# A Mamba-2 and stick-breaking encoder on one core: the SSD stage with GpSimd's tensor operations moved to VectorE, both PSUM halves added directly, and the RMS scale on ScalarE

## The chip, the cores and the metric

The kernel runs on one core of one Trainium2 chip. The metric is device time of one execution in microseconds (us), as the median of several executions. The engines have short names in the profile: PE is TensorE's matmuls, PEld its weight loads, DVE is VectorE, ACT is ScalarE, POOL is GpSimd, SP is SyncE, which issues most of the transfers. Each engine works through its own queue in order.

## The reference, cut to what matters

One sequence of 512 tokens, width 1024, two layers, all in float32. Layer 0 is a Mamba-2 mixer (the SSD stage) and a squared-ReLU MLP; layer 1 is stick-breaking attention and another MLP; each of the four sub-layers ends in a LayerNorm of `alpha * h + sublayer(h)`. The change touches only the mixer:

```python
y_diag = jnp.einsum("bcgls,bcgrls,bcsgrp->bclgrp", cb, decay_mat, xc)
...
y_off = jnp.einsum("bclgn,bcgrpn,bcgrl->bclgrp", cc, prev, jnp.exp(a_cs))
return (y_diag + y_off).reshape(b, l, h, p).astype(x.dtype)
...
y = (y + xh * d_skip[:, None]).reshape(b, l, D_INNER)
yg = (y * jax.nn.silu(z)).astype(jnp.float32).reshape(b, l, SSM_GROUPS, D_INNER // SSM_GROUPS)
yg = yg * lax.rsqrt(jnp.mean(jnp.square(yg), axis=-1, keepdims=True) + RMS_EPS)
y = (yg.reshape(b, l, D_INNER) * norm_w.astype(jnp.float32)).astype(u.dtype)
return y @ w_out
```

There are 8 groups of 4 heads with 64 channels each, so a group has 256 channels.

## The kernel before, in words

**Precision.** TensorE multiplies in a rounded float32 type. To keep float32 accuracy every operand is split into a high part (a cast) and a low part (the rest), and a product is three matmuls: high by high, low by high, high by low (`mm3`, L206 to L209). So every operand costs a cast, mostly on ScalarE, and a subtraction, mostly on VectorE. Weights arrive as tiles of 128x1024 through SP's queue; `emit_w` casts them on ScalarE (`wh`, L190) and subtracts (`wl`, L192). While `extra[3]` is set, every fourth weight's subtraction (`i % 4 == 1`) goes to GpSimd and the others to VectorE. `extra[3]` is set from the start of the program until attention begins.

**The SSD stage** (`ssm`) walks over the 8 groups. The projections of the next group (`in_bc`, `in_x`: tiles `pB`, `pC`, `px`) and of this group's gate (`in_z`: `pz`) are cut into small steps, which `fill.run` strews between the steps of this group's scan. The scan has four chunks of 128 tokens. For a chunk c:
- `decays`: GpSimd masks the log decays (`dm`, L771), TensorE sums them (`sg`), ScalarE exponentiates (`dec`, L777).
- `scores`: the C-by-B products `cb`, evicted by ScalarE (`cbm`, L787) and masked by GpSimd (L788).
- `front`: `dec` times `cbm` (L799), on VectorE for chunks 0 to 2 and on GpSimd for chunk 3; the split into `W` high and low (L801, L802); the chunk's state `st`; the running state `prev` times the block decay on GpSimd (L810), plus `st` on VectorE (L812); its split `pr` (L815, L816).
- `back`: the contribution of the state `po`, scaled by VectorE into `yg` (L831), plus the skip term `dx` on GpSimd (L832); the diagonal product `py`, in two halves of 256 columns side by side in one PSUM tile; ScalarE copies the second half to SBUF (`yl`, L840), GpSimd adds it to `yg` (L841), VectorE adds the first half from PSUM (L842).
- `gate` multiplies by silu(z) on VectorE (L847) and squares with a row sum on ScalarE (`ss`, L848). `finish` makes the reciprocal root on GpSimd (L856, L857), scales the four chunks of `yg` on VectorE (L859), transposes them on TensorE (`pyt`, L864) and splits the result into `yT` (L867, L868).

After groups 3 and 7 the output projection `so` runs in `tok_out` (L298 and L300 add it into the residual `v`). After the stage come MLP, attention and the second MLP.

**What sets the order.** The source order is only an input: the framework schedules every engine's queue by a timeline model of its own, over the whole program, and then puts in the semaphore waits. A change of a few instructions can therefore move others. PSUM has two sets of four buffers, `bg` for the scan's tiles and `mm` for projections.

Of the kernel before, what the change touches and what calls it, by code (L numbers as in the profile page):

```python
# [11 lines left out]
F32 = mybir.dt.float32  # L12
F32R = mybir.dt.float32r
AF = mybir.ActivationFunctionType
ALU = mybir.AluOpType
PSUM = bass.MemoryType.PSUM

P = 128
# [17 lines left out]
def trunk(ctx: ExitStack, tc: tile.TileContext, io):  # L36
    nc = tc.nc
# [7 lines left out]
    def psum(tag, shape, name):  # L45
        return ps.tile(shape, F32, tag=tag, name=name, bufs=4)
# [7 lines left out]
    def f(x):  # L54
        return x.bitcast(F32)
# [85 lines left out]
    marks.append(len(stream))  # L141
    ready = []
    taken = [0]
    extra = [None, 0, 0, True, 0]
    alt = {}
    sums = {}
    depth = [2]
# [58 lines left out]
    def mm3(out, a, b, start, stop, skip=False):  # L206
        nc.tensor.matmul(out, a[0], b[0], start=start, stop=False, skip_group_check=skip)  # L207
        nc.tensor.matmul(out, a[0], b[1], start=False, stop=False, skip_group_check=skip)  # L208
        return nc.tensor.matmul(out, a[1], b[0], start=False, stop=stop, skip_group_check=skip)  # L209
# [355 lines left out]
    def ssm(sp, nxt_ln):  # L565
# [33 lines left out]
        S4 = [P, 4, P]  # L599

        def pair(name, shape, tag, bufs):
            return tuple(sp.tile(shape, F32R, tag=tag + s, name=name + s, bufs=bufs) for s in "hl")
# [77 lines left out]
        def v3(t):  # L680
            return t.rearrange("p (h d) -> p h d", h=4)
# [111 lines left out]
        def front(q, c):  # L793
            g = q.g
            hs = slice(4 * g, 4 * g + 4)
            nm = f"{g}_{c}"
            dec = q.dec[c]
            eng = nc.gpsimd if c == 3 else nc.vector
            eng.tensor_tensor(dec, dec, q.cbm[:, c, :].unsqueeze(1).to_broadcast(S4), op=ALU.mult)  # L799
            W = q.W[c] = pair(f"W{nm}", S4, "W", 2)  # L800
            nc.scalar.copy(W[0], dec)  # L801
            nc.vector.tensor_sub(W[1], dec, f(W[0]))  # L802
            if c < NT - 1:
                pst = psum("bg", [P, 256], f"st{nm}")
                mm3(pst, (q.bt[0][:, c, :], q.bt[1][:, c, :]), (q.xe[0][:, c, :], q.xe[1][:, c, :]), True, True)
                if c == 0:
                    q.prev = sp.tile([P, 256], F32, tag="prev", name=f"pv{nm}", bufs=1)
                    nc.vector.tensor_copy(q.prev, pst)
                else:
                    nc.gpsimd.tensor_tensor(v3(q.prev), v3(q.prev),  # L810
                                            bdec[:, c, hs].unsqueeze(2).to_broadcast([P, 4, HP]), op=ALU.mult)
                    nc.vector.tensor_add(q.prev, pst, q.prev)  # L812
                nprev = q.prev
                pr = q.pr[c + 1] = pair(f"pr{nm}", [P, 256], "pr", 2)
                nc.scalar.copy(pr[0], nprev)  # L815
                nc.vector.tensor_sub(pr[1], nprev, f(pr[0]))  # L816

        def back(q, c):
            g = q.g
            hs = slice(4 * g, 4 * g + 4)  # L820
            cs = slice(c * P, (c + 1) * P)
            nm = f"{g}_{c}"
            if c == 0:
                q.yg = sp.tile([P, NT, 256], F32, tag="yg", name=f"yg{g}", bufs=1)
                q.ss = sp.tile([P, NT], F32, tag="ss", name=f"ss{g}", bufs=2)
            W, pr = q.W[c], q.pr[c]
            yc = q.yg[:, c, :]
            if c > 0:
                po = psum("bg", [P, 256], f"po{nm}")
                mm3(po, (q.C[0][:, cs], q.C[1][:, cs]), pr, True, True)  # L830
                nc.vector.tensor_tensor(v3(yc), v3(po), E[:, c, hs].unsqueeze(2).to_broadcast([P, 4, HP]), op=ALU.mult)  # L831
                nc.gpsimd.tensor_add(yc, yc, q.dx[:, c, :])  # L832
            py = psum("bg", [P, 4, 2, HP], f"py{nm}")
            for h in range(4):
                xh = q.xd[:, c, h, :, :].rearrange("p s d -> p (s d)")
                ph = py[:, h, :, :].rearrange("p s d -> p (s d)")
                nc.tensor.matmul(ph, W[0][:, h, :], xh, start=True, stop=False)
                nc.tensor.matmul(py[:, h, 0, :], W[1][:, h, :], q.xd[:, c, h, 0, :], start=False, stop=True)
            yl = sp.tile([P, 256], F32, tag="yl", name=f"yl{nm}", bufs=1)
            nc.scalar.copy(v3(yl), py[:, :, 1, :])  # L840
            nc.gpsimd.tensor_add(yc, yl, yc if c > 0 else q.dx[:, c, :])  # L841
            nc.vector.tensor_tensor(v3(yc), py[:, :, 0, :], v3(yc), op=ALU.add)  # L842

        def gate(q, c):
            nm = f"{q.g}_{c}"
# [4 lines left out]
        def finish(q, parts=1):  # L850
            g, yg = q.g, q.yg
            n = NT // parts
            for i in range(parts):
                cs = range(i * n, i * n + n)
                ss = q.ss[:, i * n:i * n + n]
                nc.gpsimd.tensor_scalar(ss, ss, 1.0 / 256.0, RMS_EPS, ALU.mult, ALU.add)  # L856
                nc.gpsimd.tensor_tensor(ss, ss, mhalf.to_broadcast([P, n]), op=ALU.pow)  # L857
                for c in cs:
                    nc.vector.tensor_scalar(yg[:, c, :], yg[:, c, :], q.ss[:, c:c + 1], None, ALU.mult)  # L859
                for j in range(2):  # L860
                    kt = 2 * g + j
                    pt = psum("bg", [P, n * P], f"pyt{g}{j}{i}")
                    for ci, c in enumerate(cs):
                        nc.tensor.transpose(pt[:, ci * P:(ci + 1) * P], yg[:, c, j * P:(j + 1) * P], ident)  # L864
                    ts_ = slice(i * n * P, (i + 1) * n * P)
                    oh, ol = yT[0][:, kt % 8, ts_], yT[1][:, kt % 8, ts_]
                    nc.scalar.activation(oh, pt, AF.Copy, scale=nw[:, kt:kt + 1])  # L867
                    nc.vector.scalar_tensor_tensor(ol, pt, nw[:, kt:kt + 1], f(oh), ALU.mult, ALU.subtract)  # L868
# [16 lines left out]
        for g in range(G):  # L885
# [3 lines left out]
            q = cur  # L889
# [7 lines left out]
            scores(q)  # L897
            fill.run(4)
            front(q, 0)
            fill.run(5)  # L900
            front(q, 1)
            fill.run(5)
            back(q, 0)
            fill.run(4)
            front(q, 2)
            fill.run(4)
            back(q, 1)
            fill.run(4)
            front(q, 3)
            fill.run(4)  # L910
            back(q, 2)
            fill.run(4)
            back(q, 3)
# [5 lines left out]
            if nxt:  # L919
                decays(nxt)  # L920
            finish(q, 1 if nxt else 2)
            if g == G - 1:
                def in_xd(i):
# [356 lines left out]
```

## Time and profile before

| what | value |
|---|---|
| three timed executions | 1426.99, 1427.30 (the median) and 1427.46 us |
| the profiled execution, and its span from first to last instruction | 1426.79 us, 1424.7 us |
| TensorE busy | 1394.1 us, 98% of the span |
| VectorE busy | 1078.2 us, 76% |
| ScalarE busy | 783.9 us, 55% |
| GpSimd busy | 221.4 us, 16% |
| mean granted TensorE clock | 0.994 of full speed |

The profile is one execution. A row of a group gives line, engine, operation, output and inputs, shape, count, then the engine's busy time, the mean time of one in ns, and the idle time of the engine before it with what ended it. A row of the timeline gives start and length. Matmuls are pipelined, so their lengths overlap, and the distance from one start to the next is what a matmul costs. GpSimd's work lies in the first 450 us, which are the SSD stage; after that it is nearly idle.

### The profile page before, as it was taken

The numbers are of one execution on the slowest core, as the hardware profiler recorded it, in microseconds if no ns is written. First come the engines' busy times: TensorE is split into PE (matmuls) and PEld (weight loads), VectorE is DVE, ScalarE is ACT, GpSimd is POOL, SyncE is SP. The second block draws the span as 40 slices with busy tenths as digits, with TensorE's granted clock in tenths as the row PEclk, the third lists the DMA queues.
The fourth block names the chain that finished last, engine by engine and source line by source line (L and its number), as shares of the span: only waits on it lengthen the run. The fifth ranks groups of instructions, "written<-read, shape, count | busy, mean of one in ns | idle before, by whom it ended". The sixth has DMA issues, their size and how long they took to land. (4 is left out here: it accounts for less than half of the span.)

```text
span 1424.7 us, 19323 instructions
## 1 busy us (share of the span) xinstructions
PE 1394.1 (98%) x7414; PEld 1199.9 (84%) x7414; DVE 1078.2 (76%) x1530; ACT 783.9 (55%) x1264; POOL 221.4 (16%) x249
## 2 busy tenths in 40 slices
PE   9999999999999999999999899999999999999996
PEld 6898897889997988888888789899878888888885
DVE  5798898368877695876849868787867876858587
ACT  5556574246653453626345468898842735454453
POOL 2344555135443100000000200000000000000001
PEclk9999999999999999999999999999999999999999
DMA  5223212221223356455443421121223455454533
GB/s 185 75 77 131 75 60 75 89 89 60 75 75 104 125 157 179 132 179 161 148 148 120 146 89 38 52 75 45 89 75 118 131 165 162 149 175 136 176 111 126
DMA packets 46699, 162.99 MB, mean 114 GB/s; under 512 B 5520, under 2 KB 5776, under 8 KB 46608
## 3 DMA queue, kind: packets, MB, share of 16 engines
q1 hardware_dynamic: 44016, 157.44, 35.4%
q10 hardware_dynamic: 2592, 4.33, 1.0%
q8 instruction: 58, 0.95, 0.3%
q14 instruction: 33, 0.27, 0.1%
HBM read 159.65 MB, written 2.10 MB: 114 GB/s over the span
## 5 line engine op out<-in xcount | busy, mean ns | idle before, releaser
L190 ACT CAST wh<-wr 128x1024 fp32r<-128x1024 f32 x235 | 246.7, 1050 | 328.5 <-DMA wr<-w 165.1
L192 DVE TENSOR_TENSOR wl<-wr,wh 128x1024 fp32r<-128x1024 f32 x218 | 268.4, 1232 | 184.3 <-ACT wh L190 182.9
L208 PE MATMUL f<-ln_hl,wh 128*128 128x512 f32 (+1 forms) x544 | 201.2, 371 | 0.0
L209 PE MATMUL f<-ln_hh,wl 128*128 128x512 f32 (+1 forms) x544 | 201.1, 370 | 0.0
L207 PE MATMUL f<-ln_hh,wh 128*128 128x512 f32 (+1 forms) x544 | 200.4, 371 | 0.0
L208 PEld LDWEIGHTS f<-ln_hl,wh 128*128 128x128 f32 x544 | 102.3, 188 | 17.6 <-DVE ln_hl L399 0.2
L209 PEld LDWEIGHTS f<-ln_hh,wl 128*128 128x128 f32 x544 | 102.3, 188 | 17.4
L207 PEld LDWEIGHTS f<-ln_hh,wh 128*128 128x128 f32 x544 | 101.9, 188 | 17.5
L347 POOL TENSOR_TENSOR ln_rs<-ln_sums 128x1 f32<-128x1 f32 (+1 forms) x6 | 3.1, 523 | 635.3 <-ACT lnr L345 635.3
L208 PE MATMUL X<-wl,hP 128*128 128x512 f32 x192 | 74.7, 389 | 0.0
L207 PE MATMUL X<-wh,hP 128*128 128x512 f32 x192 | 74.7, 389 | 0.0
L209 PE MATMUL X<-wh,l 128*128 128x512 f32 x192 | 74.2, 390 | 0.2 <-DVE l L460 0.2
L209 PE MATMUL pz<-wh,x_l 128*128 128x256 f32 x256 | 72.8, 284 | 0.0
L208 PE MATMUL pz<-wl,x_h 128*128 128x256 f32 x256 | 72.6, 284 | 0.0
L207 PE MATMUL pz<-wh,x_h 128*128 128x256 f32 x256 | 72.5, 283 | 0.0
L459 ACT CAST hP<-r 128x512 fp32r<-128x512 f32 x80 | 48.1, 620 | 32.4 <-DVE r L471 31.5
L192 POOL TENSOR_TENSOR wl<-wr,wh 128x1024 fp32r<-128x1024 f32 x17 | 42.5, 2503 | 93.3 <-ACT wh L190 92.9
L207 PE MATMUL px<-x_h,wh 128*128 128x512 f32 x128 | 50.8, 397 | 0.0
L208 PE MATMUL px<-x_l,wh 128*128 128x512 f32 x128 | 50.2, 393 | 0.0
L209 PE MATMUL px<-x_h,wl 128*128 128x512 f32 x128 | 50.2, 392 | 0.0
L208 PE MATMUL Y<-wl,hP 128*128 128x512 f32 x128 | 49.8, 389 | 0.0
L208 PEld LDWEIGHTS pz<-wl,x_h 128*128 128x128 f32 x256 | 48.7, 190 | 0.9
(1365 smaller groups left out, 3930.7 us busy)
## 6 DMA issues: line engine op xcount, KB each, us to landing
wr<-w SPq DMA_DIRECT2D x160, 512.0 KB, 3.6
wr<-w_bc SPq DMA_DIRECT2D x16, 512.0 KB, 3.6
wr<-w_x SPq DMA_DIRECT2D x16, 512.0 KB, 3.6
wr<-w_z SPq DMA_DIRECT2D x16, 512.0 KB, 3.5
wr<-w_so SPq DMA_DIRECT2D x16, 512.0 KB, 3.6
rawa<-w SPq DMA_DIRECT2D x16, 512.0 KB, 3.6
rawc<-w SPq DMA_DIRECT2D x16, 512.0 KB, 4.5
wr<-w_qk SPq DMA_DIRECT2D x16, 512.0 KB, 3.6
```

Source lines behind the costliest of these rows:

```text
L190: nc.scalar.copy(hi, raw)
L192: eng.tensor_sub(lo, raw, f(hi))
L207: nc.tensor.matmul(out, a[0], b[0], start=start, stop=False, skip_group_check=skip)
L208: nc.tensor.matmul(out, a[0], b[1], start=False, stop=False, skip_group_check=skip)
L209: return nc.tensor.matmul(out, a[1], b[0], start=False, stop=stop, skip_group_check=skip)
L347: nc.gpsimd.tensor_add(rs, self.sq[:, t0:t1, 0], self.sq[:, t0:t1, 1])
L459: nc.scalar.copy(h, src)
```

## The change

Six edits. GpSimd's share of the weight subtractions, the product for chunk 3, the decay of the running state and the addition of the skip term go to VectorE. The second half of `py` is no longer copied to SBUF and added by GpSimd: VectorE adds both halves from PSUM, the first one together with what stood in `yg` (or `dx` in chunk 0). The RMS scale of `yg` goes from VectorE to ScalarE. GpSimd keeps the masks (L771, L788) and the reciprocal root.

```diff
-    extra = [None, 0, 0, True, 0]
+    extra = [None, 0, 0, False, 0]
...
-            eng = nc.gpsimd if c == 3 else nc.vector
-            eng.tensor_tensor(dec, dec, q.cbm[:, c, :].unsqueeze(1).to_broadcast(S4), op=ALU.mult)
+            nc.vector.tensor_tensor(dec, dec, q.cbm[:, c, :].unsqueeze(1).to_broadcast(S4), op=ALU.mult)
...
-                    nc.gpsimd.tensor_tensor(v3(q.prev), v3(q.prev),
+                    nc.vector.tensor_tensor(v3(q.prev), v3(q.prev),
                                             bdec[:, c, hs].unsqueeze(2).to_broadcast([P, 4, HP]), op=ALU.mult)
...
-                nc.gpsimd.tensor_add(yc, yc, q.dx[:, c, :])
+                nc.vector.tensor_add(yc, yc, q.dx[:, c, :])
...
-            yl = sp.tile([P, 256], F32, tag="yl", name=f"yl{nm}", bufs=1)
-            nc.scalar.copy(v3(yl), py[:, :, 1, :])
-            nc.gpsimd.tensor_add(yc, yl, yc if c > 0 else q.dx[:, c, :])
-            nc.vector.tensor_tensor(v3(yc), py[:, :, 0, :], v3(yc), op=ALU.add)
+            nc.vector.tensor_tensor(v3(yc), py[:, :, 0, :], v3(yc if c > 0 else q.dx[:, c, :]), op=ALU.add)
+            nc.vector.tensor_tensor(v3(yc), py[:, :, 1, :], v3(yc), op=ALU.add)
...
-                    nc.vector.tensor_scalar(yg[:, c, :], yg[:, c, :], q.ss[:, c:c + 1], None, ALU.mult)
+                    nc.scalar.activation(yg[:, c, :], yg[:, c, :], AF.Copy, scale=q.ss[:, c:c + 1])
```

The number of matmuls stays at 7,414, but the scheduler orders most of the stage anew. Line numbers of the changed kernel are one lower than before from L799 to L838 and three lower from L847 on; its two additions of `py` are L838 and L839.

**VectorE at the start of the program.** `x_l` is the low part of the input x (eight tiles), `wl` that of a weight. Before:

```order
L577 TENSOR_TENSOR wdtlo<-wdt,wdthi 128x8x32
L590 TENSOR_TENSOR x_l<-xf,x_h 128x512
L192 TENSOR_TENSOR wl_130<-wr_127,wh_129 128x1024
L590 TENSOR_TENSOR x_l<-xf,x_h 128x512 x7
L192 TENSOR_TENSOR wl_238<-wr_235,wh_237 128x1024
```

With the change:

```order
L577 TENSOR_TENSOR wdtlo<-wdt,wdthi 128x8x32
L590 TENSOR_TENSOR x_l<-xf,x_h 128x512
L192 TENSOR_TENSOR wl_130<-wr_127,wh_129 128x1024
L590 TENSOR_TENSOR x_l<-xf,x_h 128x512 x3
L192 TENSOR_TENSOR wl_139<-wr_136,wh_138 128x1024
L590 TENSOR_TENSOR x_l<-xf,x_h 128x512 x4
L192 TENSOR_TENSOR wl_238<-wr_235,wh_237 128x1024
```

The weight `wl_139`, which GpSimd made before, now stands between the fourth and the fifth `x_l`.

**TensorE at the same place.** `pdt` and `pB` use x tile by tile, `pC` uses the weight 138/139. Before:

```order
L207 MATMUL pC_290<-x_h,wh_138 128x512
L208 MATMUL pC_290<-x_l,wh_138 128x512
L207 MATMUL pdt<-x_h,wdthi 128x512
L207 MATMUL pB_241<-x_h,wh_129 128x512
L208 MATMUL pdt<-x_l,wdthi 128x512
L209 MATMUL pdt<-x_h,wdtlo 128x512
```

With the change:

```order
L207 MATMUL pC_290<-x_h,wh_138 128x512
L208 MATMUL pC_290<-x_l,wh_138 128x512
L207 MATMUL pdt<-x_h,wdthi 128x512
L207 MATMUL pB_241<-x_h,wh_129 128x512
L209 MATMUL pC_290<-x_h,wl_139 128x512
L207 MATMUL pC_290<-x_h,wh_138 128x512
```

Where `pdt` asked for the fifth `x_l`, `pC` now goes on with the new weight: eleven matmuls of `pC` come before the next one that needs the fifth `x_l`.

**VectorE at the end of group 3,** just ahead of the output projection. `py_3` is the diagonal product of chunk 3, `pxt` the transposed x of group 4, `sz` the gate. Before:

```order
L842 TENSOR_TENSOR yg_2117<-py_3_2339,yg_2117 128x256
L847 TENSOR_TENSOR yg_2117<-yg_2117,sz_2318 128x256
L192 TENSOR_TENSOR wl_2546<-wr_2543,wh_2545 128x1024
L672 SCALAR_TENSOR_TENSOR ca_x_2407<-px_2382,cw,ca_x_2407 128x511
L859 TENSOR_SCALAR yg_2117<-yg_2117,ss_2118 128x256 x4
L672 SCALAR_TENSOR_TENSOR ca_x_2407<-px_2382,cw,ca_x_2407 128x510
L672 SCALAR_TENSOR_TENSOR ca_x_2407<-px_2382,cw,ca_x_2407 128x509
L729 TENSOR_TENSOR dx_2416<-pxt_2417,hv 128x512
L732 TENSOR_TENSOR xt_2423<-pxt_2417,dt 128x512
```

With the change:

```order
L838 TENSOR_TENSOR yg_2093<-py_3_2309,yg_2093 128x256
L192 TENSOR_TENSOR wl_2574<-wr_2571,wh_2573 128x1024
L729 TENSOR_TENSOR dx_2384<-pxt_2385,hv 128x512
L732 TENSOR_TENSOR xt_2391<-pxt_2385,dt 128x512
L839 TENSOR_TENSOR yg_2093<-py_3_2309,yg_2093 128x256
L729 TENSOR_TENSOR dx_2384<-pxt_2398,hv 128x512
L732 TENSOR_TENSOR xt_2404<-pxt_2398,dt 128x512
L844 TENSOR_TENSOR yg_2093<-yg_2093,sz_2288 128x256
```

The gate of the last chunk (L847 before, L844 now) stands behind the work on both `pxt` tiles; before it stood ahead of them, and so did the scale. On TensorE, the last `py_3` is followed before the change by 89 matmuls of 512 columns and the eight transposes of `pxt` until the first `pyt`, and with it by 26 and the same eight: first the four into the first `pxt` tile, then ten of the 26, then the four into the second, then the other 16.

## The prediction

> **What bounds the kernel now.** I read the page first, then the busy time by stretches, then TensorE's waits.
>
> ```profile
> span 1424.7 us, 19323 instructions
> PE 1394.1 (98%) x7414; PEld 1199.9 (84%) x7414; DVE 1078.2 (76%) x1530; ACT 783.9 (55%) x1264; POOL 221.4 (16%) x249
> ```
>
> TensorE is busy for 98% of the span and the change takes no matmul from it. So the change can only move the 30.6 us in which TensorE is idle (1424.7 - 1394.1), and of these only those in the start and the SSD stage. The stretches below are the stage, its first half (from the transposed x of group 0 to that of group 4) and its second half; columns are the length, then busy time of PE, PEld, DVE, ACT and POOL, then the granted clock, the share of DMA and GB/s.
>
> ```profile
> 35.60:463.00 427.40, 420.88 (x2530) 372.05 (x2529) 341.02 (x538) 230.88 (x406) 183.70 (x187) 1.00 0.26 82
> 61.70:230.10 168.40, 166.47 (x1032) 148.59 (x1031) 149.54 (x240) 103.29 (x189) 82.21 (x85) 1.00 0.25 79
> 230.10:408.30 178.20, 175.60 (x1063) 156.13 (x1061) 131.91 (x200) 91.93 (x156) 71.39 (x71) 1.00 0.26 78
> ```
>
> TensorE idles for 6.5 us of the stage. VectorE is close behind: 89% busy in the first half (149.54 of 168.40), 74% in the second. The waits of TensorE in the first 500 us, each with its total, its number and its longest:
>
> ```profile
> PE so L207 <- DVE v L298: 1.6, 1, 1.6
> PE pdt L208 <- DVE x_l L590: 1.6, 2, 1.4
> PE pyt L864 <- DVE yg L859: 1.4, 1, 1.4
> PE so L207 <- DVE v L300: 1.3, 1, 1.3
> PE st L207 <- ACT dec L777: 1.0, 1, 1.0
> PE po L207 <- DVE pv L812: 0.4, 1, 0.4
> PE py L838 <- DVE W_0l L802: 0.2, 1, 0.2
> ```
>
> These seven come to 7.5 us. Nearly all end on VectorE. That is the whole stock from which a gain can come: 0.5% of the time.
>
> **What GpSimd costs VectorE now.** The groups of VectorE in the stage; the count, busy time, mean ns of one:
>
> ```profile
> L192 DVE TENSOR_TENSOR wl<-wr,wh 128x1024 fp32r<-128x1024 f32 x49 | 61.8, 1261 | 45.7 <-ACT wh L190 45.4
> L799 DVE TENSOR_TENSOR dec<-dec,cbm 128x512 f32<-128x512 f32 x24 | 23.5, 1028 | 1.0 <-POOL cbm L788 1.0
> L842 DVE TENSOR_TENSOR yg<-py,yg 128x256 f32<-128x256 f32 x32 | 13.2, 413 | 7.0 <-POOL yg L841 7.0
> L859 DVE TENSOR_SCALAR yg<-yg,ss 128x256 f32<-128x256 f32 x32 | 11.5, 419 | 4.7 <-POOL ss L857 4.7
> L831 DVE TENSOR_TENSOR yg<-po,E 128x256 f32<-128x256 f32 x24 | 9.9, 412 | 2.3 <-PE po L209 2.3
> L802 DVE TENSOR_TENSOR W_3l<-dec,W_3h 128x512 fp32r<-128x512 f32 x8 | 9.6, 1201 | 0.0
> L802 DVE TENSOR_TENSOR W_2l<-dec,W_2h 128x512 fp32r<-128x512 f32 x8 | 8.2, 1026 | 0.0
> L802 DVE TENSOR_TENSOR W_1l<-dec,W_1h 128x512 fp32r<-128x512 f32 x8 | 7.5, 940 | 0.0
> L816 DVE TENSOR_TENSOR pr_1l<-pv,pr_1h 128x256 fp32r<-128x256 f32 x8 | 6.5, 809 | 1.7 <-ACT pr_1h L815 1.7
> L802 DVE TENSOR_TENSOR W_0l<-dec,W_0h 128x512 fp32r<-128x512 f32 x8 | 5.8, 730 | 0.0
> ...
> 79.45 2.56 DVE L802 TENSOR_TENSOR W_2l<-dec,W_2h 128x512 fp32r<-128x512 f32 x1
> 79.06 2.40 POOL L192 TENSOR_TENSOR wl<-wr,wh 128x1024 fp32r<-128x1024 f32 x1 [0.21 <-ACT wh L190]
> ```
>
> The same subtraction of 128x512 takes 730 ns for `W_0l` and 1201 ns for `W_3l`; one `W_2l` took 2.56 us, and it ended at 82.01, 0.55 us after GpSimd's `wl` did (79.06 + 2.40 = 81.46). So VectorE stood still until GpSimd was through. Instructions with an input in PSUM (L842, L831) show nothing of it: 413 and 412 ns. [...]
>
> I estimate the sum of this standing still against about 680 ns for 512 columns (730 is the nearest row, still a little stretched) and 412 for 256: L799 24 x 0.35 = 8.4 us; the four L802 groups 8 x (0.52 + 0.35 + 0.26 + 0.05) = 9.4; `pr_1l` 8 x 0.40 = 3.2. That is 21 us. Groups that I don't show may add up to half as much again: 21 to 32 us over the stage, half of it in each half.
>
> **The change part by part.**
>
> ```profile
> L192 POOL TENSOR_TENSOR wl<-wr,wh 128x1024 fp32r<-128x1024 f32 x14 | 35.4, 2525 | 55.5 <-ACT wh L190 55.2 <-ACT yl L840 0.3
> L832 POOL TENSOR_TENSOR yg<-yg,dx 128x256 f32<-128x256 f32 x24 | 20.8, 868 | 22.3 <-DVE yg L831 22.1
> L810 POOL TENSOR_TENSOR pv<-pv,bdec 128x256 f32<-128x256 f32 x16 | 13.7, 859 | 32.3 <-DVE pr_0l L816 15.4 <-DVE pr_1l L816 14.2 <-PE st L208 2.8
> L799 POOL TENSOR_TENSOR dec<-dec,cbm 128x512 f32<-128x512 f32 x8 | 13.0, 1626 | 0.7
> L840 ACT COPY yl<-py 128x256 f32<-128x256 f32 x32 | 11.7, 366 | 14.8 <-POOL yg L841 10.3 <-PE py L838 4.5
> L848 ACT ACTIVATE sz<-yg 128x256 f32<-128x256 f32 x32 | 13.3, 415 | 16.7 <-DVE yg L847 16.4
> L848 ACT ACTIVATION_READ_ACCUMULATOR sz<-yg 128x1 f32 x32 | 6.0, 187 | 0.0
> ```
>
> *VectorE gets* 14 weight subtractions (1.26), 8 products (0.68), 16 decays, 24 skip additions and 32 second halves of `py` (0.41 each): 17.6 + 5.4 + 6.6 + 9.8 + 13.1 = 52.5 us. The second half of `py` has the first half's own row, L842. The trace has no decay or skip addition on VectorE: they are bounded by the 256-column rows, 0.41 alone and 0.81 (`pr_1l`) beside GpSimd; I take 0.41, because the GpSimd work that did the stretching is what leaves. *VectorE loses* 32 scales (13.4 us) and the standing still (21 to 32). Net: 7 to 18 us more on 341 busy of 427 us, from 80% to about 83%. In the first half 4 to 9 us more on 149.5 of 168.4, so 91 to 94%. It still fits under TensorE, but only just; the second half has ample room.
>
> *ScalarE* swaps 32 copies at 0.37 us for 32 scales. A scale from SBUF isn't in the trace; its bounds are 0.37 (L840) and 0.60 (L848 with a read of its sum), and I take 0.42. That is 2 us more on 231 of 427 us: hidden. It is a new step in the chain to `pyt`, though, and stands in ScalarE's queue behind casts.
>
> *Dependent chains.* From `py` to the end of `yg` it was copy, GpSimd addition, VectorE addition; now two VectorE additions. All transposes, projections and state products of the other groups lie beside it, so what counts is whether TensorE waits. I go through its waits.
>
> 1. *Start.*
>
> ```profile
> 14.11 3.91 DVE L590 TENSOR_TENSOR x_l<-xf,x_h 128x512 fp32r<-128x512 f32 x4 [2.95 <-ACT x_h L589]
> 13.27 2.39 POOL L192 TENSOR_TENSOR wl<-wr,wh 128x1024 fp32r<-128x1024 f32 x1 [9.32 <-ACT wh L190]
> 14.46 0.40 PE L207 MATMUL pB<-x_h,wh 128*128 128x512 f32 x1
> 16.26 0.50 PE L208 MATMUL pdt<-x_l,wdthi 128*128 128x512 f32 x1 [1.40 <-DVE x_l L590]
> ```
>
> The fifth `x_l` stood still behind GpSimd's `wl` until 15.7, so TensorE got it at 16.26 in place of 14.69 (0.23 after 14.46). With the change VectorE makes this `wl` itself in its idle time before 14.11: from about 13.3 to 14.5. TensorE then does eleven matmuls of `pC`, 2.5 us, while the fifth `x_l` is ready at about 15.1. The wait goes: **-1.5 us**. None of the other waits in the list belongs to the start or to group 0, so the head start is kept.
>
> 2. *Group 1*, `py` and `po` (0.2 + 0.4): both came after L799 and L802 instructions that stood still. **-0.6.**
>
> 3. *Group 2*, `pyt` behind L859: scale and `pyt` now stand later in the order, with more of the filler between, and the scale no longer queues on VectorE. **-1.4.**
>
> 4. *Group 3*, a new wait. The order shows 26 matmuls of 512 columns (0.23 each) and eight transposes between `py_3` and the first `pyt`: at 0.11 (estimated as half of 0.23): about 6.9 us in which the whole chain has to pass; before it was some 21 us (89 of them and the transposes). The chain: VectorE's L838 (0.41), but then the gate stands behind the second `pxt`, which TensorE reaches only after four transposes, ten matmuls and four more: 3.2 us after `py_3`. Two instructions on it (about 0.7 each, by `W_0l`) and the gate (0.41) end at 5.0; square and sum (0.60) 5.6; GpSimd's two steps, from the rows
>
> ```profile
> 219.21 0.82 POOL L856 TENSOR_SCALAR ss<-ss 128x4 f32<-128x4 f32 x1 [2.29 <-ACT sz L848]
> 220.11 1.03 POOL L857 TENSOR_TENSOR ss<-ss,mhalf 128x4 f32<-128x4 f32 x1
> ```
>
> 1.9 us, 7.5; scales at 0.42, 7.9 for the first and about 9 for the fourth. TensorE comes at 6.9, and its eight `pyt` end at about 9.2 in place of 7.8: a wait of 1 to 2 us, more where ScalarE's casts stand ahead of the scale. I take **+1.4**. What is queued behind it on TensorE are `cb`, `st` and the end of the projection `so`, which all need it or wait for the same engines anyway.
>
> 5. The waits of `so` on L298 and L300 and of `st` on `dec` (3.9 together) end on VectorE's and ScalarE's queues just behind the last group; VectorE has one L799, one decay and a `wl` more there, and fewer stretched ones. I leave them: **0**, with -3.9 to +3 for the range.
>
> Sum: -1.5 - 0.6 - 1.4 + 1.4 = -2.1 us. The profiled execution took 1426.79, so 1424.7; the median lies 0.5 above it, so **1425.2 us**, 0.15% below 1427.3.
>
> **The rivals.**
>
> *(a) The waits on VectorE go as well (faster).* For it: the waits on L298, L300 and `dec` end on VectorE or just behind it, and VectorE loses 21 to 32 us of standing still. If the new wait in group 3 stays away and half of the 3.9 goes: -3.5 - 2 = -5.5, so 1421.8. Against it: 52.5 us of instructions come in.
>
> *(b) VectorE becomes the bound of the first half (slower).* The place is groups 0 to 3. GpSimd keeps its masks, and they read SBUF as well:
>
> ```profile
> L771 POOL TENSOR_SCALAR_AFFINE_SELECT dm_2l<-da_l 128x512 fp32r<-128x512 f32 x8 | 8.7, 1088 | 1.3 <-PE sg L775 1.1
> ```
>
> There are eight such masks (this one has the longest mean) and one of `cbm` in each group. If VectorE, now denser, stands still for these in place of the old ones, nothing is freed: 149.5 + half of 39.1 (52.5 - 13.4) = 169.1 us of work in 168.4. It decides from where VectorE passes 100%, since then every product waits for it; at 2 to 4 us beyond, with the gains at the start kept or lost, the time is 1429 to 1433, say 1431. [...] Against it: the masks already run beside VectorE before, their part of the stretch is small next to that of GpSimd's long `wl`, and the second half can't be bound.
>
> *(c) Nothing in total.* The new order trades waits for waits: 1427.3.
>
> **How the numbers follow.** A measurement of this kernel can tell about 0.2% (2.9 us) from no change, so faster means below 1424.4 and slower above 1430.2. Forecast 0.45 (its own range 1423.5 to 1427, a quarter of it below 1424.4), (a) 0.27, (b) 0.18, (c) 0.10. Faster: 0.27 + 0.11 = 0.38. Same: 0.34 + 0.10 = 0.44. Slower: 0.18. The range from 1421 to 1431 takes in most of (a) and half of (b).
>
> **What would show it.** Right: `W_3l`, L798 and `pr_1l` near 0.68 and 0.41 us; no TensorE wait at 16 us; VectorE's busy time in the stage at 348 to 359 us; a wait of `pyt` near 235 us with ScalarE's L856 behind it. Wrong: VectorE over 97% in groups 0 to 3 and TensorE waiting on `W`, `pr` or `wl` there (b); TensorE's idle time in the stage under 3 us (a). Moved order in MLP or attention, where I count nothing, could also shift a microsecond.

## The result and the profile after

| kernel | median | executions | lowest to highest |
|---|---|---|---|
| before | 1427.14 us | 20 | 1423.84 to 1428.36, and one of 3583.37 |
| changed | 1429.91 us | 20 | 1426.61 to 1431.35 |

The ratio is 1.0017, with a 95% interval of 1.0010 to 1.0024 (the execution of 3583.37 us is not in it): the change makes the kernel slower, by 2.8 us between the medians and by 0.17% (2.4 us) by the ratio. The forecast was 1425.2 us, so the sign was wrong. The time lies inside the range (1421 to 1431). The profiled execution of the changed kernel took 1430.99 us, 4.2 us more than that of before; how 4.2 and 2.8 go together comes out below.

What the change was meant to do, it did. The first fence is the head of the page of the changed kernel, the second the busy times by stretches (length, PE, PEld, DVE, ACT, POOL, granted clock, DMA share, GB/s), the third groups of VectorE and the scale on ScalarE.

```profile
span 1429.0 us, 19288 instructions
PE 1400.0 (98%) x7414; PEld 1206.9 (84%) x7414; DVE 1085.4 (76%) x1596; ACT 787.9 (55%) x1264; POOL 96.5 (7%) x151
```

```profile
35.60:463.00 427.40, 423.01 (x2523) 374.57 (x2522) 344.58 (x600) 233.90 (x406) 66.62 (x92) 0.99 0.26 82
61.70:230.10 168.40, 168.40 (x1038) 150.53 (x1037) 152.30 (x271) 103.30 (x183) 26.12 (x36) 1.00 0.26 84
```

```profile
L798 DVE TENSOR_TENSOR dec<-dec,cbm 128x512 f32<-128x512 f32 x32 | 20.1, 683 | 0.6 <-POOL cbm L788 0.6
L831 DVE TENSOR_TENSOR yg<-yg,dx 128x256 f32<-128x256 f32 x24 | 10.0, 418 | 0.2
L801 DVE TENSOR_TENSOR W_3l<-dec,W_3h 128x512 fp32r<-128x512 f32 x8 | 5.5, 682 | 0.0
L815 DVE TENSOR_TENSOR pr_1l<-pv,pr_1h 128x256 fp32r<-128x256 f32 x8 | 3.3, 418 | 0.9 <-ACT pr_1h L814 0.9
L737 DVE TENSOR_TENSOR xt<-xt,dec_s 128x512 f32<-128x512 f32 x8 | 8.0, 996 | 0.0
L856 ACT ACTIVATE yg<-yg,ss 128x256 f32<-128x256 f32 x32 | 13.8, 498 | 9.6 <-POOL ss L854 9.6
```

`W_3l` fell from 1201 to 682 ns and `pr_1l` from 809 to 418. (L737, of which more below, stayed near its 1034 ns of before.) VectorE took 62 more instructions in the stage and is busy 3.6 us longer (344.58 against 341.02). In the first half of the stage TensorE is now busy for all 168.40 us at the full clock. The loss is elsewhere, and the waits of TensorE show where (same columns as before: total, number, longest):

```profile
PE f L208 <- DVE ln_hl L399: 2.6, 1, 2.6
PE sg L774 <- POOL dm_2h L771: 1.6, 1, 1.6
PE sg L775 <- POOL dm_2l L771: 1.4, 1, 1.4
...
PE so L207 <- ACT yT4h L864: 0.5, 1, 0.5
PE so L207 <- DVE v L300: 0.3, 1, 0.3
...
PE sg L774 <- POOL dm_3h L771: 0.2, 1, 0.2
```

All seven waits that the prediction listed are gone or down to 0.3 us in this profile. Two new places have come: `sg` behind GpSimd's masks near 233 us, and the MLP's `f` behind the low part of the LayerNorm's output near 473 us. The windows around both show what follows (same columns as the stretches; the cuts are those of the trace's own clock records, 3.413 us apart):

```profile
231.96:235.37 3.41, 0.64 (x2) 0.19 (x1) 3.41 (x5) 3.06 (x8) 2.97 (x4) 1.00 0.00 0
235.37:238.78 3.41, 2.92 (x9) 2.23 (x10) 1.51 (x2) 1.68 (x4) 2.64 (x4) 0.50 0.57 161
238.78:242.20 3.42, 3.42 (x17) 3.25 (x16) 1.41 (x2) 1.88 (x4) 0.63 (x1) 0.50 0.00 0
242.20:245.61 3.41, 3.41 (x11) 2.73 (x11) 2.64 (x6) 2.08 (x4) 0.64 (x1) 0.50 0.00 0
245.61:249.02 3.41, 3.41 (x17) 2.81 (x16) 2.19 (x6) 0.00 (x0) 0.00 (x0) 1.00 0.00 0
...
470.89:474.30 3.41, 0.84 (x7) 0.75 (x7) 3.41 (x7) 0.76 (x2) 0.00 (x0) 1.00 0.61 221
474.30:477.71 3.41, 3.41 (x18) 3.41 (x18) 2.77 (x6) 0.00 (x0) 1.85 (x2) 0.50 0.99 364
```

In the first and the sixth row TensorE works for 0.64 and 0.84 of 3.41 us. Each is followed by windows at half the granted clock: three behind the first, one behind the second. TensorE looks fully busy in them, but gets through 11 matmuls where it does 17 at full clock (fourth and fifth row): of the `so` matmuls of 512 columns one starts every 0.43 us at half clock (242.58 to 245.14) and every 0.23 us behind it (245.82 to 248.55). So each of the two waits is paid for twice, the second time where no view of waits shows it. The heads of the two pages say the same: with the same 7,414 matmuls TensorE is busy for 5.9 us more than before (1400.0 against 1394.1) and idle for 1.6 us less (29.0 against 30.6).

**Where the time went.** For every matmul I take the distance from the start of the one before, less the median distance of that pair of shapes over all traces (227 ns between two of 512 columns). What is left is time lost, by waiting or by a low clock. Summed by stretches, in us, for the profiled execution of each kernel (the experiments e1 to e9 follow below):

| kernel | start, to 35.6 | group 1, 106-142 | group 2, 142-178 | end of group 3, 214-250 | end of stage, 428-463 | 463-500 | rest | sum |
|---|---|---|---|---|---|---|---|---|
| before | 5.8 | 1.3 | 1.8 | 3.6 | 3.6 | 0.4 | 21.4 | 37.9 |
| changed | 4.5 | 0.2 | 0.3 | 9.2 | 1.7 | 5.0 | 21.0 | 41.9 |
| e1 | 4.5 | 0.2 | 0.3 | 9.1 | 2.1 | 0.4 | 21.1 | 37.7 |
| e2 | 5.9 | 0.4 | 1.7 | 3.0 | 1.2 | 0.4 | 20.2 | 32.8 |
| e3 | 4.8 | 0.3 | 0.2 | 2.4 | 1.7 | 6.1 | 21.9 | 37.4 |
| e4 | 4.4 | 0.4 | 0.4 | 4.4 | 1.7 | 0.4 | 22.2 | 33.9 |
| e5 | 4.9 | 0.2 | 0.4 | 11.2 | 2.6 | 0.4 | 19.4 | 39.2 |
| e6 | 4.9 | 0.3 | 0.3 | 6.1 | 2.1 | 0.4 | 19.1 | 33.2 |
| e7 | 4.8 | 0.4 | 1.8 | 2.8 | 1.3 | 0.3 | 19.1 | 30.4 |
| e8 | 4.4 | 0.3 | 0.2 | 7.2 | 1.7 | 5.0 | 20.8 | 39.6 |
| e9 | 5.0 | 0.3 | 0.3 | 7.2 | 1.7 | 5.0 | 19.0 | 38.6 |

From before to changed the sum grows by 4.0 us, of the 4.2 between the two executions. The change gains 5.8 us (start 1.3, group 1 1.1, group 2 1.5, end of the stage 1.9) and loses 10.3 (5.6 at the end of group 3, 4.6 behind the stage).

**Why at the end of group 3.** Two pieces of the changed kernel's timeline, TensorE and then the engines that it waits for (start, length, engine; in brackets the idle time and who ended it):

```profile
231.71 0.39 PE L775 MATMUL sg<-dm_1l,tri_gt 128*128 128x512 f32 x1
233.71 0.50 PE L774 MATMUL sg<-dm_2h,tri_gt 128*128 128x512 f32 x1 [1.61 <-POOL dm_2h L771]
235.62 0.79 PE L775 MATMUL sg<-dm_2l,tri_gt 128*128 128x512 f32 x1 [1.40 <-POOL dm_2l L771]
236.65 0.79 PE L774 MATMUL sg<-dm_3h,tri_gt 128*128 128x512 f32 x1 [0.24 <-POOL dm_3h L771]
237.24 1.48 PE L861 MATMUL pyt<-ident,yg 128*128 128x128 f32 x6
```

```profile
225.96 0.42 DVE L838 TENSOR_TENSOR yg<-py,yg 128x256 f32<-128x256 f32 x1
230.37 0.56 DVE L844 TENSOR_TENSOR yg<-yg,sz 128x256 f32<-128x256 f32 x1
...
231.73 0.42 ACT L845 ACTIVATE sz<-yg 128x256 f32<-128x256 f32 x1
234.83 1.71 ACT L856 ACTIVATE yg<-yg,ss 128x256 f32<-128x256 f32 x4 [0.34 <-POOL ss L854]
...
229.43 0.63 POOL L771 TENSOR_SCALAR_AFFINE_SELECT dm_1h<-da_h 128x512 fp32r<-128x512 f32 x1 [21.84 <-PE sg L774]
...
232.33 0.28 POOL L853 TENSOR_SCALAR ss<-ss 128x4 f32<-128x4 f32 x1 [1.68 <-ACT sz L845]
232.68 0.97 POOL L771 TENSOR_SCALAR_AFFINE_SELECT dm_2h<-da_h 128x512 fp32r<-128x512 f32 x1
233.63 1.17 POOL L854 TENSOR_TENSOR ss<-ss,mhalf 128x4 f32<-128x4 f32 x1
234.77 0.80 POOL L771 TENSOR_SCALAR_AFFINE_SELECT dm_2l<-da_l 128x512 fp32r<-128x512 f32 x1
```

The whole chain from the last `py` to the scale has to pass while TensorE works off the few matmuls that stand behind that `py`. When they are through (231.94, 0.23 after the start of the last `sg_1`), GpSimd has just got the sum of squares; from then on it makes masks and root by turns, and TensorE waits for the masks. It starts the first `pyt` at 237.24, 5.3 us later, with three `sg` in between (0.7 us at 0.23).

Two things make the masks late. They have one buffer (`pair(f"dm{nm}", S4, "dm", 1)`), so a mask can be made only when the `sg` of the chunk before has read its own: GpSimd waited for `sg` ahead of `dm_1h`, and `dm_2h` needs the first `sg_1`. So `sg` that stand next to one another in the order are not ready work. And GpSimd is slower here: `dm_1h` took 0.63 us, the next three masks 0.97, 0.80 and 1.08, with VectorE's two-input instructions on SBUF (L737, L192, L740) beside them. Neither was tried by itself.

**Why behind the stage.** VectorE's queue around the second addition of `so` (L300), first before, then changed; `ln_hl` is what `f` needs:

```profile
467.52 0.68 DVE L300 TENSOR_TENSOR v<-so,v 128x512 f32<-128x512 f32 x1
468.24 0.69 DVE L302 BATCH_NORM_STATS2 ln_st<-v 128x6 f32<-128x512 f32 x1
468.85 0.67 DVE L399 TENSOR_TENSOR ln_hl<-ln_b,ln_hh 128x512 fp32r<-128x512 f32 x1
469.44 0.20 DVE L351 BATCH_NORM_AGGREGATE ln_mv<-ln_st 128x2 f32<-128x12 f32 x1
469.55 1.23 DVE L399 TENSOR_TENSOR ln_hl<-ln_b,ln_hh 128x512 fp32r<-128x512 f32 x2
```

```profile
469.75 1.23 DVE L192 TENSOR_TENSOR wl<-wr,wh 128x1024 fp32r<-128x1024 f32 x1
470.89 0.69 DVE L302 BATCH_NORM_STATS2 ln_st<-v 128x6 f32<-128x512 f32 x1
471.50 1.40 DVE L360 SCALAR_TENSOR_TENSOR v<-v,ln_mv,lnr 128x512 f32<-128x512 f32 x2
472.81 2.48 DVE L399 TENSOR_TENSOR ln_hl<-ln_b,ln_hh 128x512 fp32r<-128x512 f32 x4
```

The first `ln_hl` came at 468.85 and now comes at 472.81, because a `wl`, a statistic and two instructions of the LayerNorm stand ahead of it. No edit touches this place.

### The profile page after: what moved, and what is told of

Read it like the earlier page. It is cut to its first block, busy times and chain, and to the rows that moved or that the text cites. A ratio compares the mean times of both kernels' runs of the same rounds, so it can differ in the third digit from the quotient of the medians.

```text
span 1429.0 us, 19288 instructions
## 1 busy us (share of the span) xinstructions
PE 1400.0 (98%) x7414; PEld 1206.9 (84%) x7414; DVE 1085.4 (76%) x1596; ACT 787.9 (55%) x1264; POOL 96.5 (7%) x151
## 5 line engine op out<-in xcount | busy, mean ns | idle before, releaser
L192 DVE TENSOR_TENSOR wl<-wr,wh 128x1024 fp32r<-128x1024 f32 x235 | 288.0, 1227 | 199.8 <-ACT wh L190 199.4
L207 PE MATMUL Y<-wh,hP 128*128 128x512 f32 x128 | 49.5, 389 | 0.0
L207 PEld LDWEIGHTS pz<-wh,x_h 128*128 128x128 f32 x256 | 48.7, 190 | 0.7
```

Source lines behind the costliest of these rows:

```text
L192: eng.tensor_sub(lo, raw, f(hi))
```

## The experiments

I held three theories. **A**: the loss is these two waits and the half clock behind each. **B**: VectorE has become too dense (rival (b) of the prediction). **C**: the clock falls anyway, and only the waits count.

**e1: the scale back on VectorE.** The order keeps the end of group 3 as it is and puts `ln_hl` back among the additions.

```diff
-                    nc.scalar.activation(yg[:, c, :], yg[:, c, :], AF.Copy, scale=q.ss[:, c:c + 1])
+                    nc.vector.tensor_scalar(yg[:, c, :], yg[:, c, :], q.ss[:, c:c + 1], None, ALU.mult)
```

> The changed kernel with one edit undone: VectorE does the RMS scale again. The order of TensorE and GpSimd around the end of group 3 stays what it is in the changed kernel (35 matmuls between the last py of group 3 and its first pyt, the reciprocal root between the masks dm_1, dm_2 and dm_3), but the four ln_hl after the stage stand again among the additions, ahead of the second pair of L360. Theory A (the loss is two waits of TensorE, of sg for masks at 232 to 237 us and of f for ln_hl at 473 us, each followed by a stretch at half the granted clock): the first stays, with about 4 us of waiting and a clock record of 0.5 behind it; the second goes, with its 2.6 us of waiting and 3.4 us at half clock (1.7 us lost); so 1429.9 - 4.3 = about 1425.6. Theory B (a denser VectorE costs the time): VectorE gets 32 scales of 0.42 us back, 13 us more, so the time is 1430 or above. Theory C (the granted clock falls anyway, wherever the kernel is): only the wait goes, 1427.3.

Measured: 1425.87 us, ratio to before 0.9989 (0.9980 to 0.9998). In the table the stretch from 463 to 500 us falls from 5.0 to 0.4 and the end of group 3 stays at 9.1. So the second wait costs some 4 us, and more work on VectorE makes the kernel faster, not slower: B falls (VectorE is busy for 354.8 us of the stage here, against 344.6), and C with its 1427.3 too. It also shows that group 2's gain (0.3 in both) does not need the scale to move.

**e2: weights and decay left on GpSimd.** In this order 97 matmuls stand between the last `py` of group 3 and its first `pyt`, against 34 in the changed kernel (the 26 and the eight of the section on the change). The expectations count the first `pyt` in, so each of their counts is one higher.

```diff
-    extra = [None, 0, 0, False, 0]
+    extra = [None, 0, 0, True, 0]
...
-                    nc.vector.tensor_tensor(v3(q.prev), v3(q.prev),
+                    nc.gpsimd.tensor_tensor(v3(q.prev), v3(q.prev),
```

> The changed kernel with two edits undone: GpSimd subtracts its share of the weights again and decays the running state again. In this order 98 matmuls stand between the last py of group 3 and its first pyt (35 in the changed kernel), GpSimd does the reciprocal root ahead of all the masks of the next group's chunks 1 to 3, and ln_hl stands among the additions. Theory A: no wait of sg for a mask near 235 us, no wait of f for ln_hl at 473 us, no clock record of 0.5 in the stage; the wait for x_l at 16 us is back (+1.3); of the relief in groups 1 and 2 at least half stays: 1425 to 1427. Theory B: VectorE has 24 instructions of the 52 us fewer; the time falls in proportion to VectorE's load, to about 1428.5. Theory C: 1425, with the same clock as in the changed kernel.

Measured: 1421.94 us, ratio 0.9962 (0.9949 to 0.9974). Both losses are gone (3.0 and 0.4) and the start's 1.3 us is back, as A had it; but it came out 3 us below A's 1425, since I had left out that the waits of `so` and `st` go as well (the end of group 3 and the end of the stage together lose 3.0 us less than before). Group 2's gain is not there (1.7): the wait of `pyt` is gone, but `sg` waits 0.7 us for `dm_2h`, which stands behind a root that waited 3.5 us for its square. It is the same queue as in group 3, in another place.

**e3: filler matmuls in the wait.** Twelve matmuls more, whose sums are overwritten.

```diff
+                if g == 4 and c in (2, 3):
+                    for _ in range(6):
+                        nc.tensor.matmul(pseg, tri_gt, q.B[0].rearrange("p (a s) -> p a s", a=4), start=True, stop=True)
                 nc.tensor.matmul(pseg, tri_gt, dm[0], start=True, stop=False)
```

> The changed kernel with twelve matmuls of 512 columns added, whose result is overwritten: six ahead of each of sg_2 and sg_3 of group 4. They stand between the two sg_1 of the changed order, where TensorE waits for GpSimd's masks, and take 12 x 0.227 = 2.7 us of TensorE's time. Nothing else moves but four of the pyt. Theory A (the idle time at 232 to 237 us costs as much again by the clock that is granted behind it): the fillers only fill idle time, TensorE never idles for over 2 us in a row there, the clock record of 0.5 behind it (10.2 us long in the profiled execution of the changed kernel) goes, and the kernel with more work is faster: 1429.9 - 4 = about 1426. Rival (the clock has nothing to do with the wait): the fillers fill the wait and nothing else changes, 1429.9; where they push sg and pyt back, up to 1432.

Measured: 1426.77 us, ratio to before 0.9999 (0.9990 to 1.0008), so 3.1 us faster than the changed kernel with 2.7 us more work. Its timeline and its windows there:

```profile
231.95 2.88 PE L776 MATMUL sg<-B4h,tri_gt 128*128 128x512 f32 x12
234.67 0.39 PE L778 MATMUL sg<-dm_1l,tri_gt 128*128 128x512 f32 x1
234.90 0.39 PE L777 MATMUL sg<-dm_2h,tri_gt 128*128 128x512 f32 x1
235.64 1.13 PE L864 MATMUL pyt<-ident,yg 128*128 128x128 f32 x3 [0.35 <-ACT yg L859]
```

```profile
233.06:236.48 3.42, 2.92 (x13) 1.82 (x12) 3.42 (x5) 2.80 (x7) 3.33 (x4) 1.00 0.09 14
236.48:239.89 3.41, 3.41 (x23) 2.89 (x24) 2.05 (x3) 2.86 (x6) 2.00 (x4) 1.00 0.41 142
```

The first `pyt` starts at 235.64, where it was 237.24. TensorE is idle for 0.5 us of the window and not for 2.8, and the next window has the full clock. The fillers are not all that changed: four `pyt` moved, so that the first one stands ahead of the second `sg_2` and no longer behind the first `sg_3`, and it starts 1.6 us earlier. Without the clock that could give 1.6 us at most, so 1428.3; the median lies 1.5 below that. How much is the clock's is shown without any edit by e8 and e9.

**e4: the weights and the two halves of `py` alone.** Of the six edits the other four are undone (product, decay, skip addition, scale). The order has 88 matmuls between the last `py` of group 3 and its first `pyt`.

> Two edits alone: VectorE subtracts all weights, and both halves of py are added from PSUM. 89 matmuls stand between the last py of group 3 and its first pyt, GpSimd does the reciprocal root ahead of the masks, ln_hl stands among the additions. Theory A: the wait for x_l at 16 us is gone (-1.3), no long wait of sg or f, no new clock record of 0.5 in the stage, part of the relief in groups 1 and 2: 1424 to 1425.5, faster than the kernel before. Theory B: VectorE gets 17.6 + 13.1 = 30.7 us and loses nothing but stretch, the densest VectorE of these four, so it is slower than the kernel before.

Measured: 1421.22 us, ratio 0.9961 (0.9948 to 0.9973), faster than A had it: start, groups 1 and 2 and the end of the stage gain 5.6 us, the last of which (1.9) I had left out. VectorE is given 30.7 us of instructions here (350.5 us busy in the stage, against 341.0 before) and the kernel is faster than before: B is out. One part of the expectation failed: there is a new stretch at half clock in the stage, one window at 244.84 us, behind a window with 2.12 us of idle time in which `so` waits for `v` (L298); that wait is 2.1 us here and 1.6 before. So the end of group 3 loses 4.4 us and not 3.6.

**e5: the second half of `py` by copy again.** Three masks ahead of the root, but only 29 matmuls between `py` and `pyt`.

```diff
-            nc.vector.tensor_tensor(v3(yc), py[:, :, 0, :], v3(yc if c > 0 else q.dx[:, c, :]), op=ALU.add)
-            nc.vector.tensor_tensor(v3(yc), py[:, :, 1, :], v3(yc), op=ALU.add)
+            yl = sp.tile([P, 256], F32, tag="yl", name=f"yl{nm}", bufs=1)
+            nc.scalar.copy(v3(yl), py[:, :, 1, :])
+            nc.gpsimd.tensor_add(yc, yl, yc if c > 0 else q.dx[:, c, :])
+            nc.vector.tensor_tensor(v3(yc), py[:, :, 0, :], v3(yc), op=ALU.add)
```

> The changed kernel with one edit undone: ScalarE copies the second half of py and GpSimd adds it. In this order GpSimd makes the masks dm_1 and dm_2 of the next group and dm_3h ahead of the reciprocal root, but only 30 matmuls stand between the last py of group 3 and its first pyt, and ln_hl stands among the additions. This tells two readings of the wait at 232 to 237 us apart. A1 (too few matmuls stand behind the last py to cover the chain through gate, square, root and scale; GpSimd's order decides only who waits): TensorE waits just as long, 3 us or more, but at pyt for yg, a clock record of 0.5 follows, and the time is that of the kernel with the scale back on VectorE, about 1426. A2 (the root that stands between the masks is the cause): no window of 3.4 us there has over 1 us of idle time, no record of 0.5 follows, and the time is about 1422.

Measured: 1429.8 us, ratio 1.0025 (1.0015 to 1.0034). Its waits of TensorE:

```profile
PE pyt L863 <- ACT yg L858: 1.5, 1, 1.5
PE sg L775 <- POOL dm_3l L771: 1.4, 1, 1.4
...
PE sg L774 <- POOL dm_2h L771: 0.7, 1, 0.7
...
PE sg L775 <- POOL dm_2l L771: 0.5, 1, 0.5
PE sg L774 <- POOL dm_3h L771: 0.5, 1, 0.5
```

The wait is spread over `sg` and `pyt`, comes to 4.6 us, and has a stretch at half clock behind it. So a root between the masks is not needed for the loss (A2 falls): too few matmuls stand behind `py`. A1 had that right, but not the place: 3.1 of the 4.6 us are still waits for masks, 1.7 of them for the three that stand ahead of the root. GpSimd began `dm_2h` only at 232.43, having waited 1.52 us for the `sg` that reads the mask before it. A1's size failed too (1426): the stretch lost 11.2 us, with the copy and GpSimd's addition in the chain.

**e6: both losses taken away.** The edits of e1 and e3 together.

> Both losses taken away at once: the changed kernel with the RMS scale back on VectorE (which puts ln_hl back among the additions) and with the twelve filler matmuls between the two sg_1. If the two losses of theory A are all there is and independent of each other, it gains what each run gained alone: 1429.9 - 4.0 - 3.1 = 1422.8, with no record of 0.5 in the first 500 us, and so it lies below the kernel before by the relief that the other edits brought (start 1.3, groups 1 and 2 2.4, end of the stage 1.9, less 2.7 of fillers and what is left of the wait). If there is a further loss that the comparison hid, it stays at 1425 or above.

Measured: 1422.67 us, ratio 0.9972 (0.9963 to 0.9981). The median is what the gains of the two runs add up to (1422.8). One expectation failed: the profiled execution (1424.62 us) still has a stretch at half clock near 238 us, since the scales on VectorE let `pyt` wait and a window has 1.75 us of idle time.

**e7: a version that beats both.** e2, with only the first of GpSimd's weights taken from it (17 subtractions become 16).

```diff
-        eng = nc.gpsimd if extra[3] and i % 4 == 1 else nc.vector
+        eng = nc.gpsimd if extra[3] and i % 4 == 1 and i > 2 else nc.vector
```

> The kernel with weight subtractions and decay left on GpSimd, but the program's first weights (up to the third) subtracted by VectorE. The order behind the start stays the same. The wait of pdt for x_l at 16 us goes, 1.3 us: 1421.9 - 1.3 = 1420.6, the fastest so far. [...]

Measured: 1419.74 us, ratio 0.9956 (0.9942 to 0.9969), 6.8 us below the kernel before in the same comparison (1426.54) and 2.2 below e2 (1.7 when each is taken against its own comparison). In no window of its stage is TensorE idle for more than 1.2 us, and its stage has no record of half clock.

**e8 and e9: the changed kernel twice more**, for the place of the clock's grid.

> The changed kernel unaltered, for a second trace. In the traces so far the clock records lie on a grid of 3.413 us, and the records of 0.5 follow a grid window in which TensorE idled for about 1.4 us or more in all. If that is how it works, the waits of this execution are those of the first one (sg 1.6, 1.4 and 0.2 us near 233 us, f 2.6 us near 471 us), while the grid lies elsewhere against them: each record of 0.5 follows a window with at least 1.3 us of idle time, none follows one with less, and the number of such records, not the waits, makes the difference in time to the first trace (1.7 us for each 3.4 us at half clock). If the clock follows something else, there are records of 0.5 that no such window precedes.

> As the run before, a third trace of the changed kernel at another place of the grid; the same is expected of it.

Measured, one execution each: 1428.56 and 1427.57 us. The long waits are the same (1.6, 1.4 and 2.6 us in both); that of `sg` for `dm_3h` is 0.5 and not 0.2. The windows of e9 near 233 us:

```profile
231.02:234.43 3.41, 1.80 (x9) 1.18 (x7) 3.07 (x6) 3.40 (x8) 1.66 (x4) 1.00 0.02 7
234.43:237.85 3.42, 1.48 (x6) 0.78 (x7) 3.01 (x4) 2.81 (x7) 3.42 (x4) 1.00 0.36 95
237.85:241.26 3.41, 3.41 (x18) 3.23 (x16) 0.85 (x2) 1.75 (x3) 1.30 (x3) 0.50 0.17 66
```

Here the grid cuts the wait in two halves of 1.6 and 1.9 us of idle time; half clock follows for one window, not for three as in the first execution, and the stretch loses 7.2 us and not 9.2. The program is the same and so are the long waits; so 2.0 us is what two more windows at half clock cost here. I had expected 1.7 for each. Against what I expected, the first of these windows, with 1.6, has no half clock behind it.

## Why the prediction was wrong, step by step

- *What can move* ("only the 30.6 us in which TensorE is idle"): this premise failed. TensorE's idle time fell by 1.6 us and its busy time rose by 5.9, because more of the work ran at half clock (seven windows between 20 and 1410 us, three before). No term of the sum had a place for that.
- *VectorE's load*: nearly right. 344.58 us of busy time lie a little below the 348 to 359 forecast. In the groups that the prediction priced, the standing still went entirely (682 and 418 ns against the 680 and 412 taken; the skip addition 418, taken at 0.41): the product with `cbm` took from 676 to 2877 ns before (L799, median 680) and takes from 675 to 692 now (L798). Rival (b) did not come. VectorE beside GpSimd's masks is still slower here and there: six of the eight L737 of 128x512 took 1.00 to 1.12 us, each with a mask beside it, and two took 0.69, one of them with nothing of GpSimd beside it; their mean is 996 ns, where L798, with nothing of GpSimd beside any of its 32, takes 683 for the same shape. The 64 `dm` masks take from 0.63 to 1.44 us. What makes the one wait for the other was not shown. But no group shown above except L737 has a mean over 683 ns, so VectorE was relieved all the same.
- *Start* (-1.5): -1.3. *Group 1* (-0.6): -1.1. *Group 2* (-1.4): -1.5, but moving the scale is not needed for it: e1, with the scale on VectorE, keeps the gain, and e2 and e7, with the scale on ScalarE, lack it. In those two the wait of `pyt` is gone as well, and one of `sg` for a mask (0.7 us in both) has come. The kernels that have the gain (e1, e3, e4, e5, e6) share that GpSimd subtracts no weights; that this is the cause was not tried alone.
- *Group 3* (+1.4): this is **the step that failed**. The place was right and the late chain was seen, down to the gate, whose end I put 5.0 us behind `py` (225.96 to 230.93: 5.0). The mistake was to count all 26 matmuls of 512 columns as ready work. Seven of them are sums of masks, and the last three of these (both of `sg_2` and the first of `sg_3`) stand together at the end and wait for GpSimd, in whose queue the masks stand next to the very root that the chain goes through. So the cover was shorter, a mask went in between the two steps of the root, and TensorE waited 4.6 us up to the first `pyt` (5.3 less 0.7) and not 1.4. The second part of the mistake is the price: I took a wait to cost its own length. The stretch lost 5.6 us net; the waits of `so` on L298 and of `st` that went from it made 2.9 by the same distances, so the new loss is 8.5. Of this 4.6 is the wait, and the other 3.9 is the half clock behind it (by the distances of 0.43 and 0.23 us, an estimate, 10.24 us at half clock do the work of 5.5, and some of that time TensorE would have idled anyway). e9 shows the wait by itself: at full clock up to the first `pyt` it cost 4.4 us. e3 shows it by filling the wait.
- *Item 5* (0, with -3.9 to +3): the waits of `so` and `st` fell as rival (a) had it: 1.9 us at the end of the stage and the 2.9 just named. This gain lies beyond the far end that I had given it, and I took it at nothing.
- *Moved order outside the stage* ("could also shift a microsecond"): +4.6 us between 463 and 500 us, in a place that no edit touches. e1 removes it with one edit and no other change there. The order has it with all six edits; in none of the six kernels with one edit undone do all four `ln_hl` stand behind the two L360.

In the profiled execution the new wait and its half clock cost 7.1 us more than forecast (8.5 against 1.4) and the place behind the stage 4.6; item 5 gave back 4.8 and group 1 another 0.5. The prediction's range held only because gains that it had put at nothing paid for losses that it had not counted.

What shortens the cover is the scheduler. Between the last `py` of group 3 and its first `pyt` the order of each edit alone has 61 to 100 matmuls, the kernel before 97, the six kernels with one edit undone 29 to 48, the changed kernel 34 (of these twelve kernels with one edit or five, only e1 and e5 were timed). Shorter chains on VectorE let its timeline model place `pyt` earlier and use up the projection `so` before; the chain on the chip is longer than the place it leaves. That it is the model's durations that do this is argued from the orders, and was not tried by itself.

## What to carry to other kernels

Don't price a wait by its length alone, not even where TensorE is busy for 98% of the time as here. Look up the records of the granted clock in the kernel's own trace, add up TensorE's idle time between them, and see what follows. In these traces 1.42 us or more in a window of 3.413 us stood ahead of each stretch at half clock, and each window at half clock (one to three were seen) can cost 1.6 us, an estimate from the distances of 0.43 and 0.23 us. Here seven waits of 0.2 to 1.6 us went or shrank, two places with waits of 4.6 and 2.6 us came, and the kernel took 1429.91 us in place of 1427.14.

Where a scheduler orders the program, each edit moves the order everywhere. Count what stands behind the last producer before its consumer, take out of that count everything that waits for the same chain, the same queue or a buffer that it holds, and look at places that the change doesn't touch; then take the edits that leave the cover in place (here e7) and not all of them.

## What the runs showed of the hardware

In each of the eleven traces the records of TensorE's granted clock start on one grid of 3.413 us, and between 20 and 1410 us a stretch at half clock (0.50 of full speed) lasted 3.413, 6.827 or 10.240 us, one to three windows. The grid lies elsewhere in the program in each execution: the first window at half clock behind the wait at the end of group 3 starts at 235.37, 236.44 and 237.85 us in the three executions of the changed kernel. Between 20 and 1410 us the traces have 4,409 windows at full clock. 37 of them are followed by half clock, and in each of the 37 TensorE was idle for 1.42 us or more, in one wait or several: the kernel before has two of them (1.59 and 1.78 us), the first execution of the changed kernel five (1.50 to 2.77 us). Of the 4,372 others one had 1.61 us of idle time (the one in e9) and all the rest 1.37 or less. So in these traces the two kinds part near 1.4 us, with that one exception. At the end of group 3 no single wait of TensorE was longer than 1.61 us in the first execution, and half clock followed. Why three windows came in a row in three of the traces, with under 0.6 us of idle time in the second and third, was not settled.

This fits the spread of one kernel: with the same long waits, three executions of the changed kernel had 4, 5 and 7 windows at half clock between 20 and 1410 us and took 1427.57, 1428.56 and 1430.99 us, 1.0 to 1.2 us for each window more (by the distances of 0.43 and 0.23 us a window at half clock can cost 1.6, an estimate; where TensorE would wait in it anyway, it costs less). The 20 executions of the result go the same way: the three under 1428 us have a mean granted clock of 0.992 or 0.993, the nine over 1430.2 us one of 0.988 to 0.990.
